# GLA mixer: the queries also in a PSUM bank, and the gates multiplied in ahead of the norm's root

## The chip, the cores and the metric

The kernel runs on one core of a Trainium2 chip. The metric is the device time of one launch in microseconds, the median of several. TensorE does the matrix products, VectorE, ScalarE and GpSimd the element-wise work, and SyncE issues the DMAs. SBUF is the working memory; PSUM has eight banks of 128 partitions x 512 floats, into which TensorE writes. GpSimd has no operand in PSUM anywhere in this kernel.

## The reference

Two layers over 1024 tokens of width 1024: layer 0 is gated linear attention (GLA), layer 1 a Mamba-2 mixer. Each is `x + mixer(rmsnorm(x))`, and one norm ends it. The change touches layer 0 alone. With four heads, key width 128 and value width 512 for each head:

```
q, k, v, g, gk_low = split(rmsnorm(x) @ w_in)
log_a = log_sigmoid(gk_low @ w_gate_up + b) / 16
per chunk:  b = cumsum(log_a)                       # decays, per key channel
  o = (q * exp(b)) @ S + (sum_d q_i k_j exp(b_i - b_j), j <= i) @ v
  S = exp(b_last) * S + (k * exp(b_last - b))^T @ v
o = rmsnorm(o, w_head_norm) * silu(g)               # per head, over 512
y = o @ w_out
```

The reference has chunks of 64; the kernel uses 128.

## The kernel before

Activations stand with features on partitions and 512 tokens on the free axis, so the work is done in four phases: `Gla(0)`, `Gla(1)`, `Ssd(0)`, `Ssd(1)`, each for one half of the tokens. The large products take every operand as a rounded part and a rest (`wh`/`wl` for weights, `hh`/`hl` for activations, `yh`/`yl` for a mixer's output) and three matmuls (`mm3`). They come in units of 12 matmuls with 512 columns, each with one 256 KB piece of weights. A piece is loaded, rounded by ScalarE (L171) and, on its first use, its rest is formed by GpSimd (`wl`, L176); that rest is stored, and in the second half of the tokens it is read back by a DMA (L174). Pieces are prepared four units ahead.

Beside the units run "sides", Python generators that are advanced by a rate per unit. `Gla.mixer(h)` is the side of head h: it runs beside the units of `gate(h)`, `outp(h-1)` and `qkv(h+1)`, some 28 of them, at 0.95 steps for each. Its stages are:

- the gate's projection into the bank `z` (L540), its log-sigmoid and scan into `b` (L551), and a copy of `b` into the bank (L553), read from there as `bz` and `zc`;
- the decay products: `kd`, `qd` (L567) and `d` (L572 to L576), and for three block sizes `keys(s)` (L582 to L584) and `queries(s)` (L600 to L607), where differences of `b` go through `Exp` and are multiplied by `k` or `q` (L584, L604). This stretch is called the decay stage below;
- the small products (L658) of keys and queries into four banks, placed into `at` under masks (L619, L623);
- the state updates and the outputs `o` (L699 to L723);
- the tail: squares of `o` (L729), the norm's root (`rstd_steps`, left in the bank `box[0]`), the gates' `Silu` (L736), the scaling by weight and root (L741), the product with the gate on GpSimd (L742), and the split into `yh` and `yl` (L746, L747), which `outp(h)` reads in the next head's units.

PSUM is two rings of four banks: `pp` for the units, `mb` for the mixers (`z`, the transposed keys `ptk`, the four product banks, states, outputs, the root). A unit's bank is emptied by `evac` functions behind the unit; that of `outp` adds it to `accs` on VectorE (L515). In `Gla(0)` the norm's root is applied as the banks are emptied, for the gates on VectorE too (L419).

The order of the instructions on each engine is not that of the Python program. It is fixed when the kernel is built: a planner walks through the instructions by priority (earlier in the program first) with its own estimates of times and of when buffers come free, and puts each on its engine's queue as its inputs are due. On the chip each queue then runs in that order, and an instruction that waits holds up all behind it.

Of the kernel before, what the change touches and what calls it, by code (L numbers as in the profile page):

```python
# [13 lines left out]
AF = mybir.ActivationFunctionType  # L14
ALU = mybir.AluOpType

P = 128
# [25 lines left out]
C_HN = C_GB + 4  # L43
# [10 lines left out]
def hybrid_kernel(ctx: ExitStack, tc: tile.TileContext, xT, w_in0, w_gk, w_up, w_out0,  # L54
                  w_in1, w_dt, w_out1, par, masks, tri, out):
    nc = tc.nc
    V, A, G, PE = nc.vector, nc.scalar, nc.gpsimd, nc.tensor
# [13 lines left out]
    def tl(tag, bufs, shape=(P, T), dt=F32):  # L71
        cnt[0] += 1
        return sb.tile(list(shape), dt, name=f"{tag}_{cnt[0]}", tag=tag, bufs=bufs)

    def ps(tag):
        cnt[0] += 1
        return (psp if tag == "pp" else psm).tile([P, T], F32, name=f"{tag}_{cnt[0]}", tag=tag)

    def tmp(n=P):
        t = tl("t", NTMP)  # L80
        return t[:] if n == P else t[0:n, :]

    def c3(ap, w=P):
        return ap.rearrange("p (n w) -> p n w", w=w)
# [5 lines left out]
    def act(out, in_, func, **k):  # L90
        name = SILU if func == AF.Silu else LN_EXP
        i = None
        if name != table[0]:
            i = A.preload_act_table_set(name)
            for m in table[2]:
                tc.add_manual_dep(i.ins, m.ins.name, ORDER, reason="table")
            table[:] = name, i, []
        o = A.activation(out, in_, func, **k)
        tc.add_manual_dep(o.ins, table[1].ins.name, ORDER, reason="table")
        table[2].append(o)  # L100
        return o
# [32 lines left out]
    def col(c, n=P):  # L134
        return pr[0:n, c:c + 1]
# [148 lines left out]
    def rstd_steps(ssum, n, box, var=None, stay=False):  # L284

        hi, lo = tl("t", NTMP, dt=F32R)[:], tl("t", NTMP, dt=F32R)[:]
        A.copy(hi, ssum)
        V.tensor_tensor(lo, ssum, hi.bitcast(F32), op=ALU.subtract)  # L290
        p = ps("mb")
        PE.matmul(p[:], onr[:], hi, start=True, stop=False)
        PE.matmul(p[:], onr[:], lo, start=False, stop=True)
        yield
        yield from rstd_of(p, n, box, var, stay)
# [19 lines left out]
    def square_into(ss, src, first, eng):  # L315
        if first:
            A.activation(ss, src, AF.Square)
        else:
            sq = tmp()
            A.activation(sq, src, AF.Square)  # L320
            eng.tensor_tensor(ss, ss, sq, op=ALU.add)  # L321
# [87 lines left out]
    class Gla:  # L409
# [115 lines left out]
        def mixer(self, h):  # L525
            t = self.t
            q, k = self.q[h], self.k[h]
# [20 lines left out]
            b = tl("m2", 1)[:]  # L548
            for c in range(NC):
                cs = slice(c * P, (c + 1) * P)  # L550
                V.tensor_tensor_scan(b[:, cs], m[:, cs], l[:, cs], 0.0, op0=ALU.add, op1=ALU.subtract)  # L551

            A.copy(z[:], b)  # L553
            bz, zc = z[:], c3(z[:])
            yield

            bc = c3(b)
# [6 lines left out]
            yield  # L564
            qd = tl("x", 4)[:]
            act(qd, bz, AF.Exp, scale=1.0 / 16)
            V.tensor_tensor(qd, q, qd, op=ALU.mult)  # L567


            d = tmp()  # L570
            dv = c3(d)
# [1 line left out]
            act(dv[:, :, 0:64], dv[:, :, 0:64], AF.Exp, scale=-1.0 / 16)  # L573
            act(dv[:, :, 64:P], dv[:, :, 64:P], AF.Exp, scale=1.0 / 16)
            V.tensor_tensor(dv[:, :, 0:64], c3(k)[:, :, 0:64], dv[:, :, 0:64], op=ALU.mult)
            V.tensor_tensor(dv[:, :, 64:P], c3(q)[:, :, 64:P], dv[:, :, 64:P], op=ALU.mult)  # L576

            def keys(s):

# [7 lines left out]
            def queries(s, e, c0=0, c1=NC):  # L587


                w, n = 4 * s, (c1 - c0) * P // (4 * s)  # L590
                own = 4 if s == 1 else 0
                e = e[:, 0:n * (6 * s + own)].rearrange("p (n w) -> p n w", n=n)
                cs = slice(c0 * P, c1 * P)
                bv, zv, qv = c3(b[:, cs], w), c3(bz[:, cs], w), c3(q[:, cs], w)
                after = []
                for i in range(3):
                    f, l = (i + 1) * s, 4 * s
                    o = sum(4 * s - (m + 1) * s for m in range(i))
                    after.append((e[:, :, o:o + l - f], f))
                    V.tensor_tensor(after[-1][0], zv[:, :, f:l], bv[:, :, f - 1:f].to_broadcast([P, n, l - f]),  # L600
                                    op=ALU.subtract)
                act(e[:, :, 0:6 * s], e[:, :, 0:6 * s], AF.Exp, scale=1.0 / 16)
                for o, f in after:
                    V.tensor_tensor(o, qv[:, :, f:4 * s], o, op=ALU.mult)  # L604
                if own:
                    G.tensor_copy(e[:, :, 6:10], qv)
                return e.rearrange("p n w -> p (n w)")  # L607

            def place(s, p, c0=0, c1=NC):
# [17 lines left out]
            for c in range(NC):  # L627
                cs = slice(c * P, (c + 1) * P)
                PE.transpose(ptk[:, cs], kd[:, cs], ident[:])

            o2 = [tl(tag, 1, (P, 2, T))[:] for tag in ("o0", "o1")]
            flat = [x.rearrange("p n w -> p (n w)") for x in o2]
            k16, q16 = keys(16), queries(16, flat[0])
            yield
            kh, kl = tl("ktok", 1, dt=F32R)[:], tl("t", NTMP, dt=F32R)[:]
            A.copy(kh, ptk[:])
            V.tensor_tensor(kl, ptk[:], kh.bitcast(F32), op=ALU.subtract)
            yield
            k4, q4 = keys(4), queries(4, flat[1])
            yield  # L640
            v = self.v[h]
            nst = NC - 1 if t == NT - 1 else NC

            def split(c):
                if c < nst:
                    vh, vl = tl("t", NTMP, dt=F32R)[:], tl("t", NTMP, dt=F32R)[:]
                    A.copy(vh, v[c])
                    G.tensor_tensor(vl, v[c], vh.bitcast(F32), op=ALU.subtract)  # L648
                    return vh, vl

            q1 = [queries(1, tl("raw", 2, (P, N_RAW))[:], 2 * i, 2 * i + 2) for i in range(2)]
            yield

# [37 lines left out]
            o = [o2[vb // 2][:, vb % 2, :] for vb in range(4)]  # L691
            def state(c, parts):
                if c < nst:
                    p = ps("mb")
                    cs = slice(c * P, (c + 1) * P)
                    mm3(p[:], kh[:, cs], kl[:, cs], *parts, True, True)
                    return p

            pst = state(0, vp)  # L699
            vp = split(1)  # L700
            yield
            for c in range(NC):
                cs = slice(c * P, (c + 1) * P)
# [24 lines left out]
            for vb in range(4):  # L728
                square_into(ss, o[vb], vb == 0, G)  # L729
                if vb % 2:  # L730
                    yield
            yield
            box = []
            yield from rstd_steps(ss, 512, box, stay=True)
            for g in self.g[h]:
                act(g, g, AF.Silu)  # L736
            yh, yl = [], []
            self.y[h] = yh, yl
            for vb in range(4):
                u = tmp()  # L740
                V.scalar_tensor_tensor(u, o[vb], col(C_HN + vb), box[0], op0=ALU.mult, op1=ALU.mult)  # L741
                G.tensor_tensor(u, u, self.g[h][vb], op=ALU.mult)  # L742
                yield
                a = tl("yh", 6, dt=F32R)[:]
                c = tl("yl", 6, dt=F32R)[:]
                A.copy(a, u)  # L746
                V.tensor_tensor(c, u, a.bitcast(F32), op=ALU.subtract)  # L747
                yh.append(a)
                yl.append(c)


    class Ssd:
# [456 lines left out]
    box = [[] for _ in ph]  # L1209
# [29 lines left out]
    for p in range(2):  # L1239
        g = ph[p]  # L1240
        for h in range(GH):
            o = [lambda: g.outp(h - 1)] if h else ([lambda: ph[0].outp(3)] if p else [])
# [162 lines left out]
```

## Time and profile before

| | |
|---|---|
| median of 3 runs | 1612.12 us (1608.9 to 1615.64) |
| the profiled execution | 1609.57 us, its span 1607.8 us |
| TensorE busy | 1570.2 us (98%) |
| VectorE, ScalarE, GpSimd busy | 951.4, 951.4, 655.3 us |
| DMA | 309 MB, 192 GB/s over the span |

The span is what the trace covers, and the profiled execution's own time is 1.8 us longer. `Gla(0)` takes the span up to some 400 us and `Gla(1)` up to some 750 us. In the rows, a letter and number such as L604 is the line of the kernel, names to the left of `<-` are written and those to the right read; `m` is the tag of `q`, `k` and `b`, `t` and `o` of scratch tiles, `mb` and `pp` of banks. A duration that is followed by xN in a timeline is that of N instructions merged.

### The profile page before, as it was taken

What the parts mean: (1) busy time and instruction counts of PE and PEld (TensorE: products, weight loads), DVE (VectorE), ACT (ScalarE), POOL (GpSimd) and SP (SyncE); (2) the same over time, 40 slices, a digit from 0 to 9 for tenths busy, and PEclk for the clock granted to TensorE, in tenths of its full rate; (3) what the DMA queues carried; (4) which work ended last, traced back from release to release, by engine and by line L of the source; (5) the groups of instructions that cost most, each with busy time, mean ns of one, the idle gap of its engine ahead of it and who ended that gap; (6) DMA issues with size and microseconds to landing.
All of it is one profiled execution on the core that took longest, in us unless ns stands there. A gap on an engine that the chain in (4) does not pass through costs nothing.

```text
span 1607.8 us, 24028 instructions
## 1 busy us (share of the span) xinstructions
PE 1570.2 (98%) x8272; PEld 1305.0 (81%) x8272; DVE 951.4 (59%) x1579; ACT 951.4 (59%) x1796; POOL 655.3 (41%) x542
## 2 busy tenths in 40 slices
PE   7999899999999999999999999999999999999996
PEld 5787787878888888888888888888778888888886
DVE  6357567495725446386735544457976963355657
ACT  4445363544636264564865767656657777667743
POOL 6456565643411021216536656565523222222322
PEclk9999999999999999999999999999999999999999
DMA  7545465464576456464586565566665766655752
GB/s 235 194 146 156 137 195 190 132 220 161 183 268 197 151 191 202 154 200 146 174 276 202 179 199 184 181 193 222 226 198 193 240 238 217 206 177 188 259 199 85
DMA packets 172747, 309.30 MB, mean 192 GB/s; under 512 B 19089, under 2 KB 25105, under 8 KB 172625
## 3 DMA queue, kind: packets, MB, share of 16 engines
q1 hardware_dynamic: 172624, 307.77, 58.6%
q8 instruction: 65, 1.06, 0.3%
q14 instruction: 58, 0.47, 0.1%
HBM read 232.06 MB, written 75.63 MB: 191 GB/s over the span
## 4 chain that ended last, share of the span: by engine, by line
PE 78%; DVE 11%; DMA 4%; ACT 4%; issue 1%; POOL 1%; SPq 0%; DVEq 0%; ACTq 0%; POOLq 0%
PE pp L223 18%; PE pp L224 18%; PE pp L225 18%; PE pp L469 3%; PE pp L470 3%; PE pp L471 3%; DMA wraw<-w_in 2%; PE mb L956 2%; PE mb L709 2%; PE mb L708 2%; PE mb L658 1%; PE mb L949 1%; DVE o L604 1%; PE mb L223 1%; PE mb L224 1%
## 5 line engine op out<-in xcount | busy, mean ns | idle before, releaser
L171 ACT CAST wh<-wraw 128x512 fp32r<-128x512 f32 x472 | 289.4, 618 | 343.1 <-PE pp L224 164.3
L223 PE MATMUL pp<-hh,wh 128*128 128x512 f32 x1184 | 468.5, 397 | 8.8 <-ACT wh L171 7.4
L224 PE MATMUL pp<-hl,wh 128*128 128x512 f32 x1184 | 464.0, 392 | 1.3 <-DVE hl L371 1.1
L225 PE MATMUL pp<-hh,wl 128*128 128x512 f32 x1184 | 463.0, 392 | 0.0
L176 POOL TENSOR_TENSOR wl<-wraw,wh 128x512 fp32r<-128x512 f32 x240 | 328.3, 1375 | 277.1 <-ACT wh L171 232.3
L223 PEld LDWEIGHTS pp<-hh,wh 128*128 128x128 f32 x1184 | 222.8, 188 | 60.3 <-ACT wh L171 9.0
L224 PEld LDWEIGHTS pp<-hl,wh 128*128 128x128 f32 x1184 | 223.0, 188 | 48.5 <-DVE hl L371 2.5
L225 PEld LDWEIGHTS pp<-hh,wl 128*128 128x128 f32 x1184 | 222.9, 188 | 46.2
L223 PE MATMUL pp<-yh,wh 128*128 128x512 f32 x448 | 177.9, 397 | 6.1 <-DVE acc L515 5.4
L225 PE MATMUL pp<-yh,wl 128*128 128x512 f32 x448 | 175.9, 393 | 0.0
L224 PE MATMUL pp<-yl,wh 128*128 128x512 f32 x448 | 175.4, 392 | 0.0
L321 POOL TENSOR_TENSOR ss<-ss,t 128x512 f32<-128x512 f32 x53 | 74.0, 1396 | 81.8 <-ACT t L320 70.4
L223 PEld LDWEIGHTS pp<-yh,wh 128*128 128x128 f32 x448 | 84.2, 188 | 26.1 <-issue 2.8
L469 PE MATMUL pp<-wh,hh 128*128 128x512 f32 x256 | 100.4, 394 | 2.7 <-DVE m L444 2.7
L470 PE MATMUL pp<-wl,hh 128*128 128x512 f32 x256 | 100.3, 392 | 0.0
L471 PE MATMUL pp<-wh,hl 128*128 128x512 f32 x256 | 99.7, 392 | 0.0
L225 PEld LDWEIGHTS pp<-yh,wl 128*128 128x128 f32 x448 | 84.3, 188 | 18.9 <-issue 0.2
L224 PEld LDWEIGHTS pp<-yl,wh 128*128 128x128 f32 x448 | 84.2, 188 | 17.8
L827 DVE SCALAR_TENSOR_TENSOR m<-pp,pr,m 128x509 f32<-128x509 f32 (+2 forms) x96 | 70.4, 743 | 42.8 <-ACT m L824 41.7
L827 DVE SCALAR_TENSOR_TENSOR x<-pp,pr,x 128x509 f32<-128x509 f32 (+2 forms) x96 | 71.2, 743 | 32.5 <-ACT x L824 31.4
L648 POOL TENSOR_TENSOR t<-v,t 128x512 fp32r<-128x512 f32 x28 | 38.1, 1371 | 112.6 <-DMA wraw<-w_in 28.9
L1038 POOL TENSOR_TENSOR t<-t,o 128x512 fp32r<-128x512 f32 x32 | 41.8, 1310 | 91.6 <-ACT o L1036 87.0
(286 smaller groups left out, 2623.7 us busy)
## 6 DMA issues: line engine op xcount, KB each, us to landing
wraw<-w_in SPq DMA_DIRECT2D x352, 256.0 KB, 3.5
low_in<-wl SPq DMA_DIRECT2D x176, 256.0 KB, 3.8
wl<-low_in SPq DMA_DIRECT2D x176, 256.0 KB, 3.2
wraw<-w_out SPq DMA_DIRECT2D x128, 256.0 KB, 3.5
low_out<-wl SPq DMA_DIRECT2D x64, 256.0 KB, 4.0
v<-a_cum SPq DMA_DIRECT2D x64, 256.0 KB, 3.8
wl<-low_out SPq DMA_DIRECT2D x56, 256.0 KB, 3.2
xn<-x SPq DMA_DIRECT2D x43, 256.0 KB, 3.8
```

The costliest lines, as they stand in the source:

```text
L171: A.copy(hi[:, 0:w], raws[n][:, 0:w])
L176: G.tensor_tensor(lo[:, 0:w], raws[n][:, 0:w], hi[:, 0:w].bitcast(F32), op=ALU.subtract)
L223: PE.matmul(o, lh, rh, start=first, stop=False)
L224: PE.matmul(o, lh, rl, start=False, stop=False)
L225: PE.matmul(o, ll, rh, start=False, stop=last)
L321: eng.tensor_tensor(ss, ss, sq, op=ALU.add)
L469: PE.matmul(o, rh[kb][:, cs], wh[:], start=(kb == 0), stop=False)
L470: PE.matmul(o, rh[kb][:, cs], wl[:], start=False, stop=False)
L471: PE.matmul(o, rl[kb][:, cs], wh[:], start=False, stop=(kb == KB - 1))
L648: G.tensor_tensor(vl, v[c], vh.bitcast(F32), op=ALU.subtract)
L827: V.scalar_tensor_tensor(dst[:, s:], o[:, 0:T - s], col(C_CW + j * 32 + si), dst[:, s:], op0=ALU.mult, op1=ALU.add)
L1038: G.tensor_tensor(xel[-1], xe, hi.bitcast(F32), op=ALU.subtract)
```

## The change

A second bank of the `mb` ring, `qz`, gets a copy of `q` from ScalarE just behind the copy of `b`. The products of `qd`, of the second half of `d` and of all `queries` read `qz` in place of `q`; GpSimd's copy of the queries' own columns (L606) still reads `q`. The `Silu` of the gates moves up, behind the first state product. The product with the gate moves ahead of the root's computation: GpSimd multiplies `o` into the gate's own tile. Behind the root, VectorE scales that tile by weight and root and writes the result `u` to a bank of the `mb` ring, from which ScalarE and VectorE make `yh` and `yl`.

```diff
             A.copy(z[:], b)
             bz, zc = z[:], c3(z[:])
+            qz = ps("mb")[:]
+            A.copy(qz, q)
             yield
...
             act(qd, bz, AF.Exp, scale=1.0 / 16)
-            V.tensor_tensor(qd, q, qd, op=ALU.mult)
+            V.tensor_tensor(qd, qz, qd, op=ALU.mult)
...
-            V.tensor_tensor(dv[:, :, 64:P], c3(q)[:, :, 64:P], dv[:, :, 64:P], op=ALU.mult)
+            V.tensor_tensor(dv[:, :, 64:P], c3(qz)[:, :, 64:P], dv[:, :, 64:P], op=ALU.mult)
...
-                bv, zv, qv = c3(b[:, cs], w), c3(bz[:, cs], w), c3(q[:, cs], w)
+                bv, zv, qv = c3(b[:, cs], w), c3(bz[:, cs], w), c3(qz[:, cs], w)
...
                 if own:
-                    G.tensor_copy(e[:, :, 6:10], qv)
+                    G.tensor_copy(e[:, :, 6:10], c3(q[:, cs], w))
...
             pst = state(0, vp)
             vp = split(1)
+            for g in self.g[h]:
+                act(g, g, AF.Silu)
             yield
...
+            for vb in range(4):
+                G.tensor_tensor(self.g[h][vb], o[vb], self.g[h][vb], op=ALU.mult)
             yield
             box = []
             yield from rstd_steps(ss, 512, box, stay=True)
-            for g in self.g[h]:
-                act(g, g, AF.Silu)
             yh, yl = [], []
             self.y[h] = yh, yl
             for vb in range(4):
-                u = tmp()
-                V.scalar_tensor_tensor(u, o[vb], col(C_HN + vb), box[0], op0=ALU.mult, op1=ALU.mult)
-                G.tensor_tensor(u, u, self.g[h][vb], op=ALU.mult)
-                yield
+                u = ps("mb")[:]
+                V.scalar_tensor_tensor(u, self.g[h][vb], col(C_HN + vb), box[0], op0=ALU.mult, op1=ALU.mult)
                 a = tl("yh", 6, dt=F32R)[:]
                 c = tl("yl", 6, dt=F32R)[:]
                 A.copy(a, u)
                 V.tensor_tensor(c, u, a.bitcast(F32), op=ALU.subtract)
                 yh.append(a)
                 yl.append(c)
+                yield
```

## Rows read from the trace of the kernel before

**Rows 1.** the page, part 1: busy us, share of the span, instructions

```profile
PE 1570.2 (98%) x8272; PEld 1305.0 (81%) x8272; DVE 951.4 (59%) x1579; ACT 951.4 (59%) x1796; POOL 655.3 (41%) x542
```

**Rows 2.** stretch, length, busy PE, PEld, DVE, ACT, POOL (x); PEclk, DMA share, GB/s

```profile
0.00:40.00 40.00, 28.30 (x103) 20.75 (x104) 28.01 (x37) 18.47 (x33) 25.54 (x27) 0.96 0.71 236
100.00:200.00 100.00, 93.92 (x512) 79.03 (x511) 58.09 (x100) 46.83 (x87) 56.21 (x44) 1.00 0.46 147
200.00:300.00 100.00, 97.46 (x492) 80.75 (x491) 62.70 (x104) 50.79 (x91) 56.40 (x44) 0.98 0.54 175
300.00:400.00 100.00, 97.98 (x507) 79.83 (x507) 70.80 (x116) 51.11 (x92) 46.44 (x35) 1.00 0.56 180
1570.00:1608.00 38.00, 25.57 (x205) 24.67 (x203) 25.78 (x51) 11.41 (x28) 9.24 (x11) 0.90 0.26 86
```

**Rows 3.** the same view, the second head's decay stage and the second half

```profile
130.00:172.00 42.00, 35.92 (x162) 28.68 (x162) 41.50 (x63) 24.42 (x43) 27.88 (x20) 1.00 0.54 163
500.00:700.00 200.00, 200.00 (x1033) 167.64 (x1032) 99.82 (x206) 107.98 (x199) 30.79 (x27) 1.00 0.56 182
```

**Rows 4.** what TensorE waited for, 40 to 480 us: total, times, longest

```profile
PE pp L223 <- DVE acc L515: 5.4, 3, 2.3
PE mb L658 <- DVE raw L604: 4.2, 2, 3.0
```

**Rows 5.** VectorE groups by shape, 40 to 480 us

```profile
L747 DVE TENSOR_TENSOR yl<-t,yh 128x512 fp32r<-128x512 f32 x16 | 19.4, 1249 | 1.6 <-ACT yh L746 1.6
L604 DVE TENSOR_TENSOR o<-m,o 128x384 f32<-128x384 f32 x10 | 12.6, 1257 | 0.0
L604 DVE TENSOR_TENSOR o<-m,o 128x256 f32<-128x256 f32 x10 | 12.0, 1205 | 0.0
L567 DVE TENSOR_TENSOR x<-m,x 128x512 f32<-128x512 f32 x5 | 6.5, 1297 | 0.0
L600 DVE TENSOR_TENSOR o<-mb,m 128x384 f32<-128x384 f32 x10 | 5.4, 544 | 0.0
L600 DVE TENSOR_TENSOR o<-mb,m 128x256 f32<-128x256 f32 x10 | 4.1, 407 | 0.0
L637 DVE TENSOR_TENSOR t<-mb,ktok 128x512 fp32r<-128x512 f32 x5 | 3.4, 677 | 6.0 <-ACT ktok L636 6.0
```

**Rows 6.** VectorE's timeline, second head: start, length, instruction

```profile
...
139.22 1.76 DVE L747 TENSOR_TENSOR yl<-t,yh 128x512 fp32r<-128x512 f32 x1
141.50 2.89 DVE L747 TENSOR_TENSOR yl<-t,yh 128x512 fp32r<-128x512 f32 x2
...
149.95 1.78 DVE L567 TENSOR_TENSOR x<-m,x 128x512 f32<-128x512 f32 x1
...
156.24 3.48 DVE L604 TENSOR_TENSOR o<-m,o 128x384 f32<-128x384 f32 x3
...
166.33 2.69 DVE L604 TENSOR_TENSOR o<-m,o 128x384 f32<-128x384 f32 x3
168.94 2.54 DVE L604 TENSOR_TENSOR raw<-m,raw 128x192 f32<-128x192 f32 x6
...
```

**Rows 7.** two lines, 480 to 720 us: ns min/median/max, starts, shapes

```profile
L604 DVE TENSOR_TENSOR o<-m,o x18: 273/412/549, 513.8 to 707.9; 128x384 f32<-128x384 f32 x6, 128x256 f32<-128x256 f32 x6, 128x128 f32<-128x128 f32 x6
L747 DVE TENSOR_TENSOR yl<-t,yh x12: 673/678/1749, 501.9 to 685.2; 128x512 fp32r<-128x512 f32 x12
```

**Rows 8.** third head: the busy view at 256, and the chain's product matmuls

```profile
256.00:257.00 1.00, 1.00 (x7) 0.59 (x8) 1.00 (x3) 0.51 (x1) 0.00 (x0) 0.50 1.07 375
...
171.63 3.06 PE mb L658 x56
...
256.42 4.17 PE mb L658 x56
```

**Rows 9.** groups by shape, whole span: writes to a bank

```profile
L313 DVE SCALAR_TENSOR_TENSOR mb<-t,t 128x512 f32<-128x512 f32 x8 | 5.6, 700 | 0.3
...
L553 ACT COPY mb<-m 128x512 f32<-128x512 f32 x8 | 4.7, 591 | 8.3 <-DVE m L551 8.3
```

## The prediction

> **What bounds the kernel now.** I first read the page's busy times: TensorE is busy 1570.2 us of a span of 1607.8, so 37.6 us of idle time are what a change of the other engines can win at most, beside what the clock gives [rows 1]. The view by stretches then says where they lie. The first 40 us hold 11.7 us of idle and the last 38 hold 12.4, and the change touches neither the start nor the end. From 100 to 400 us TensorE loses 6.1, 2.5 and 2.0 us, together 10.6, in the decay stages of the second, third and fourth head of the first token half [rows 2]. From 500 to 700 us, the same mixer code on the second half, it is busy for the whole 200 us [rows 3].
>
> The view of waits names what TensorE stood for: 5.4 us in three waits for the adds that empty the banks of `outp` (L515), and 4.2 us in two waits for the last products with the queries (L604) [rows 4]. Both are VectorE work, and VectorE was busy 41.5 of the 42 us of the second head's decay stage [rows 3]. So in these three stretches VectorE sets the pace, and TensorE stands because its queue holds an instruction that VectorE feeds too late.
>
> Why it is late is seen in the groups by shape. The products with `q` from SBUF (L604) take 1257 ns for 384 columns and 1205 for 256; the differences of the same shapes that read one input from a bank (L600) take 544 and 407 [rows 5]. The second half shows L604 itself at 412 median and at most 549 [rows 7]. What differs is GpSimd: busy 27.9 of 42 us in the slow stretch, 30.8 of 200 in the fast one [rows 3]. I read this as VectorE instructions with two SBUF inputs standing behind a GpSimd instruction, and those with one input in a bank not standing.
>
> **The change part by part.** *Reads of `q` from the bank.* Per head, two L604 of 384 columns go from 1257 to 544 ns, two of 256 from 1205 to 407, and L567 from 1297 to the 677 of L637, which has a bank input of that size [rows 5]: 1.43 + 1.60 + 0.62 = 3.6 us.
>
> *The split from the bank.* Four L747 per head go from 1249 to 677 [rows 5]: 2.3 us. Together a mean head saves 5.9 us of VectorE. For the second head the timeline gives more: three L747 took 1.76 + 2.89 against 3 x 0.68, L567 1.78 against 0.68, and the two triples of L604 3.48 + 2.69 against two times 0.544 + 0.407 + some 0.27 (the least of L604's own times, for the 128-column one) [rows 5 to 7]. That is 2.6 + 1.1 + 3.7 = 7.4 us, and I leave the 2.54 us of the six small ones as they are.
>
> A bound from below: GpSimd's work stays, so the collisions can land on the two-SBUF instructions that remain in the stage (L563, L575, two L584). Each could lose at most what L567 lost, 1.1 us, so 4.4 us come off: 3.0 us stay in the second head and 1.5 in a mean one. I take the upper value, because fewer such instructions meet fewer collisions.
>
> What may a bank cost by itself? L600 from a bank needs 544 ns for the shape that L604 does in at most 549 from SBUF when undisturbed [rows 5, 7], so I add nothing. The Trainium skill (Perfetto Trace Analysis, "Optimizing Scalar/DVE Operations") speaks against the change here: it gives VectorE about 60 ns of access overhead on SBUF and 125 on PSUM. By it, 22 operands a head moved to banks would cost an estimated 1.4 us, and the three heads' lower bound would fall from 6.0 us to 1.8; the trace doesn't agree, and the rest goes without it.
>
> *What TensorE gets back.* VectorE is the pace-setter only while it is late. The savings (7.4, and 5.9 in a mean head) exceed the standing time of each stretch (6.1, 2.5, 2.0) [rows 2], so the waits of 9.6 us [rows 4] should go; with the lower bounds 3.0 + 1.5 + 1.5 = 6.0 us go. What speaks most for the whole is the second half, where the planner made its order of the same code, GpSimd did little, and TensorE never stood [rows 3].
>
> *The clock.* After the third head's wait the granted clock was 0.50, the 1.2 GHz level, and the 56 product matmuls took 4.17 us against 3.06 in the second head [rows 8]. Without the standing, 1.1 us come back; nothing, if the wait stays.
>
> *The copy into `qz`.* One ScalarE copy of 0.59 us per head, as L553 [rows 9]. ScalarE is busy 24.4 of 42 us [rows 3], so its time is hidden; but the copy sits ahead of the `Exp` for `kd`, and I charge 0.6 us once, to the second head, where the saving is nearest to the need. With no cover it would be 0.6 in each of three heads, 1.8.
>
> *`Silu` and the gate's product.* Four `Silu` and four GpSimd products a head are moved, not added, and the activation table still changes twice a head: before, ahead of `Silu` and of the next head's `Exp`; now ahead of `Silu` and of the root's `Ln`. The tail loses the GpSimd product between L741 and L746, but `outp(h)` first reads `yh` behind the eight units of the next gate. At 1033 matmuls in 200 us [rows 3] its 96 matmuls last over 18 us, which hides the tail already: nothing won. The scaling into a bank stays at some 0.70 us, as L313 writes one [rows 9].
>
> *Waits that are added.* The `mb` ring has four banks. `qz` holds one from the copy to the last L604, for which the first products wait already, so the product banks come no later. But ScalarE's copy must wait for a free bank, and behind it on that queue stand the `Exp` for `kd` and the roundings of weights that TensorE needs; and each `u` needs a bank, behind which VectorE's next scan stands. No DMA is added or moved past a queue.
>
> The sum: 9.6 + 1.1 - 0.6 = 10.1 us off 1609.57 gives 1599.5. The profiled execution lies 2.55 us under the median of the runs, 1612.12; against that the forecast is 1602.
>
> **The rivals.** *The planner takes the saving.* It places the product matmuls by its own estimate of when they are due. If its estimate for VectorE shrinks as the chip's does, it moves them earlier and TensorE stands there again, for what its estimate lacks. For it: TensorE stood only 2.5 and 2.0 us in heads where VectorE lost some 5.9 [rows 2, 5], so much of the lateness already fell into slack of the order. Against it: the shapes stay the same, and collisions, which the order evidently missed, are what goes. It would win 3 to 7 us: 1605 to 1609, say 1607, which is also where the lower bounds (6.0 - 0.6) end.
>
> *Nothing is won.* The standing moves to the next late thing: with VectorE faster, the chain of `Exp` on ScalarE between L600 and L604 becomes the pace, or GpSimd's rests of weights. ScalarE was idle 17.6 of the 42 us [rows 3], which speaks against it. Time: 1610 to 1613, say 1612.
>
> *The banks run out (slower).* Place: the copy into `qz`, while the tail of the head before still holds the root's bank and the `u` banks. For it: a new holder for the whole decay stage in a ring of four, and two more kinds of writers that wait on it. Against it: the splits of the tail shown end at 144.4 us, and L567, which comes behind the copy, begins only at 149.95 [rows 6], so the banks should be free. Its price: the three L747 shown run from 139.2 to 144.4, 5.2 us. If `qz` stands for that long, the saving of 5.9 is just eaten and the time stays; that is the point from which it decides. At twice that, 10.4 us, the decay stage of three heads ends 4.5 us later than now, 13.5 us: 1626. The Trainium skill ("Identifying Performance Opportunities" of the same page) says that gaps that repeat on the engine that should be full can mean too little PSUM for the next tile; before, no such gap shows between 500 and 700 us.
>
> **How the numbers follow.** The forecast has 0.60, the planner 0.25, nothing won 0.09, banks 0.06. The forecast's own range is 1597 (all 10.6 us of idle time and 1.1 of clock off the lowest run, 1608.9) to 1605. The range for 8 in 10 is 1597 to 1610: it takes in the planner's case and half of nothing won, and leaves the banks out. A measurement of this kernel can tell about 0.5%, 8.1 us, from no change, so the bound is 1604.1. Of the forecast 0.54 lies under it; the rest, the planner's case and nothing won make 0.40; the banks 0.06.
>
> **What would show it.** Right: between 40 and 480 us TensorE no longer waits for L515 and L604; L604's 384-column mean falls from 1257 to about 545 and L747's to about 680; the stretches 100 to 400 us gain about 10 us of TensorE busy time; the clock stays at its upper level near 250 us. Wrong: the same waits with a shorter L604 (the planner); waits of the ScalarE copy or of the scaling for a bank, and of TensorE for the rounded weights (the banks); or L563, L575 and L584 longer by as much as L604 got shorter.

## The result and the profile after

The changed kernel takes 1596.51 us in the median of 6 runs (1595.66 to 1600.16), against 1611.46 (1608.9 to 1615.64) for the kernel before, also in 6 runs. The ratio is 0.9912, with a 95% interval of 0.99 to 0.9924: faster by 12 to 16 us. The forecast was 1602 with a range from 1597. The direction came as said (faster by over 0.5%), and the gain is larger than said: the median lies 0.5 us under the range's lower end, while the ratio, taken from the 1612.12 us that the forecast started from, gives 1597.9, just inside it. The profiled execution took 1597.23 us, 12.3 less than that of before. Executions at a lower granted clock are left out of all ratios here, and one kernel below (`after_no_rests`) has no profile but such a one, so it gets a time and no rows.

The page's busy times, to be read against [rows 1]: the span is 1595.5 us, so TensorE's idle time went from 37.6 to 29.0 us, and its busy time fell by 3.7.

```profile
PE 1566.5 (98%) x8272; PEld 1304.9 (82%) x8272; DVE 919.1 (58%) x1579; ACT 955.2 (60%) x1804; POOL 651.2 (41%) x542
```

Busy times by stretch, in the columns of [rows 2], for the three stretches where it stood:

```profile
100.00:200.00 100.00, 98.46 (x530) 82.75 (x530) 47.51 (x102) 49.05 (x90) 54.86 (x45) 1.00 0.50 156
200.00:300.00 100.00, 100.00 (x512) 83.69 (x512) 57.77 (x104) 51.69 (x93) 65.53 (x50) 1.00 0.59 182
300.00:400.00 100.00, 100.00 (x519) 82.17 (x519) 72.41 (x132) 59.09 (x105) 41.93 (x31) 1.00 0.62 193
```

TensorE's idle time there is 1.5 us in place of 10.6, and the granted clock is at its upper level in all three. What it still waited for between 40 and 480 us, against [rows 4]:

```profile
PE pp L223 <- DVE acc L515: 1.2, 1, 1.2
PE pp L223 <- ACT yh L748: 0.3, 1, 0.3
```

Nothing waits for the products with the queries any more, and the adds of L515 cost 1.2 us in place of 5.4. VectorE's groups by shape in the same stretch, against [rows 5]; L604 is L606 now, L567 is L569, L747 is L749, and L586 is the keys' product, which still has both inputs in SBUF:

```profile
L749 DVE TENSOR_TENSOR yl<-mb,yh 128x512 fp32r<-128x512 f32 x16 | 10.6, 684 | 0.8 <-ACT yh L748 0.7
...
L586 DVE TENSOR_TENSOR t<-m,t 128x512 f32<-128x512 f32 x10 | 8.7, 873 | 0.0
...
L606 DVE TENSOR_TENSOR o<-mb,o 128x384 f32<-128x384 f32 x10 | 5.5, 548 | 0.0
...
L606 DVE TENSOR_TENSOR o<-mb,o 128x256 f32<-128x256 f32 x10 | 4.1, 411 | 0.0
...
L569 DVE TENSOR_TENSOR x<-mb,x 128x512 f32<-128x512 f32 x5 | 3.4, 683 | 0.0
```

The products with the queries take 548 and 411 ns in place of 1257 and 1205, and the split 684 in place of 1249. The chain of work in the second and third head shows the 56 product matmuls at 3.02 us each; the third took 4.17 at the lower clock before [rows 8]:

```profile
175.19 3.02 PE mb L660 x56
...
255.99 3.02 PE mb L660 x56
```

One thing came differently. The second head's gate projection (L540) opens its mixer. It started at 130.15 us before and starts at 146.81 now, the first fence being TensorE's timeline of before and the second that of after:

```profile
130.15 0.39 PE L540 MATMUL mb<-stp,wup 128*128 128x512 f32 x1
```

```profile
146.81 0.39 PE L540 MATMUL mb<-stp,wup 128*128 128x512 f32 x1
```

Its products start at 175.19 us, against 171.63 before [rows 8]. So the time from the gate projection to the products shrank from 41 to 28 us in this head, and it starts 17 us later. The planner had made another order: the projection stands behind 104 matmuls of L223 on TensorE's queue, where it stood behind 80. The tail of the head before now overlaps little on VectorE with this stage: its last split starts at 149.82 us.

Landmarks in TensorE's timeline tell where the time came off. The products of the fifth head (the first of the second token half) started at 441.8 us before and at 429.7 after, 12.1 us earlier; the sixth to eighth lead by 12.1, 10.9 and 12.1, and the end by 12.3. All of it was won by the start of the fifth head's products.

### The profile page after: what moved, and what is told of

The parts are those of the page before. It is cut to its first block, busy times and chain, and to the rows that moved or that the text cites. A ratio compares the mean times of both kernels' runs of the same rounds, so it can differ in the third digit from the quotient of the medians.

```text
span 1595.5 us, 24009 instructions
## 1 busy us (share of the span) xinstructions
PE 1566.5 (98%) x8272; PEld 1304.9 (82%) x8272; DVE 919.1 (58%) x1579; ACT 955.2 (60%) x1804; POOL 651.2 (41%) x542
## 4 chain that ended last, share of the span: by engine, by line
PE 84%; DVE 5%; ACT 5%; DMA 4%; issue 1%; POOL 1%; SPq 0%; DVEq 0%; POOLq 0%; ACTq 0%
PE pp L223 20%; PE pp L224 20%; PE pp L225 20%; PE pp L469 4%; PE pp L471 4%; PE pp L470 4%; PE mb L713 2%; PE mb L712 2%; PE mb L959 2%; PE mb L660 2%; DMA wraw<-w_in 1%; PE mb L952 1%; DMA v<-a_cum 1%; PE mb L223 1%; PE mb L224 1%
## 5 line engine op out<-in xcount | busy, mean ns | idle before, releaser
L223 PE MATMUL pp<-hh,wh 128*128 128x512 f32 x1184 | 467.9, 396 | 8.7 <-ACT wh L171 7.6
L176 POOL TENSOR_TENSOR wl<-wraw,wh 128x512 fp32r<-128x512 f32 x240 | 322.5, 1352 | 313.2 <-ACT wh L171 245.0
L223 PEld LDWEIGHTS pp<-hh,wh 128*128 128x128 f32 x1184 | 222.7, 188 | 59.5 <-ACT wh L171 9.0
L223 PE MATMUL pp<-yh,wh 128*128 128x512 f32 x448 | 177.0, 397 | 2.6 <-DVE acc L515 1.2
L223 PEld LDWEIGHTS pp<-yh,wh 128*128 128x128 f32 x448 | 84.2, 188 | 22.3 <-ACT acc L889 2.4
```

The lines of the kernel that those rows point to most:

```text
L176: G.tensor_tensor(lo[:, 0:w], raws[n][:, 0:w], hi[:, 0:w].bitcast(F32), op=ALU.subtract)
L223: PE.matmul(o, lh, rh, start=first, stop=False)
```

## The experiments

Two theories stood at the start. *Theory 1*: VectorE's instructions with two SBUF inputs stand behind GpSimd, and the change takes the queries' products and the split out of that. *Theory 2*: the planner's new order did it. All ratios below are to the kernel before, each from four or more timed runs. Beside them stands where the products of the fifth head start in the profiled execution (441.8 us before, 429.7 after), since all of the gain is made by then.

**The parts alone.** The first run (`queries_only`) is the kernel before with the queries' part of the diff, its first five hunks:

```diff
+            qz = ps("mb")[:]
+            A.copy(qz, q)
...
-            V.tensor_tensor(qd, q, qd, op=ALU.mult)
+            V.tensor_tensor(qd, qz, qd, op=ALU.mult)
...
```

The second (`tail_only`) is the changed kernel without that part:

```diff
-            qz = ps("mb")[:]
-            A.copy(qz, q)
+            qz = q
```

> The first part alone: the copy into the bank and the reads of the queries from it; the tail as before. Theory 1 (VectorE's lateness comes from its two-SBUF instructions standing behind GpSimd, and the bank takes the queries' products out of that): L604 of 384 columns falls from 1257 to about 550 ns, some 3.6 us a head, TensorE's waits between 40 and 480 us fall from 9.6 to 2 to 4 us, and the time falls by 7 to 9 us, to about 1603. Theory 2 (the new order of the planner, not the reads, took the waits away): the waits can come out anywhere, with no tie to L604's duration.

> The second part alone: Silu and the gate's product ahead of the root, the scaled output in a bank; the queries read from SBUF. Theory 1: L604 stays near 1200 ns, the split of the output falls from 1249 to about 690 ns (2.3 us a head, ahead of the decay stage); waits of 5 to 7 us are left and the time falls by 3 to 5 us, to about 1607.5. Theory 2: the tail's new order brings most of the whole, 10 us or more.

The queries alone: 1598.5 us, ratio 0.9922 (0.9905 to 0.9939). VectorE's groups and TensorE's waits, 40 to 480 us:

```profile
L749 DVE TENSOR_TENSOR yl<-t,yh 128x512 fp32r<-128x512 f32 x16 | 19.5, 1240 | 1.7 <-ACT yh L748 1.6
...
L606 DVE TENSOR_TENSOR o<-mb,o 128x384 f32<-128x384 f32 x10 | 5.5, 547 | 0.4 <-ACT o L98 0.4
```

```profile
PE pp L223 <- ACT v L478: 1.5, 2, 0.8
PE pp L223 <- DVE v L480: 1.2, 1, 1.2
PE mb L660 <- DVE raw L606: 0.2, 1, 0.2
```

L606 is at 547 ns while the split stays at 1240, and none of the old waits is left but 0.2 us. That is more than theory 1 had priced (1603): the queries' reads alone are enough for nearly all. The fifth head's products start at 431.4 us, earlier by 10.4 of the 12.1 us. And theory 2 has no part in it: set side by side, the traces of the kernel before and of this run show the same order on TensorE and GpSimd from start to end, on VectorE but for six neighbouring instructions near 410 us, and on ScalarE, the added copy apart, up to 416 us.

The traces also show the collisions one by one, by what GpSimd was running when a product started. Of the ten L604 products of 384 columns before, seven started while GpSimd was in a subtraction (L176), and they took 1049 to 1654 ns; the other three took 544 to 548. In this run again seven of ten started so, and they took 542 to 558.

The tail alone: 1601.84 us, ratio 0.9941 (0.9925 to 0.9956), where theory 1 had 1607.5. The same two views:

```profile
L748 DVE TENSOR_TENSOR yl<-mb,yh 128x512 fp32r<-128x512 f32 x16 | 10.6, 685 | 0.8 <-ACT yh L747 0.7
...
L605 DVE TENSOR_TENSOR o<-m,o 128x384 f32<-128x384 f32 x10 | 7.9, 794 | 0.0
```

```profile
PE mb L223 <- DVE a L624: 2.4, 2, 1.8
PE pp L223 <- DVE acc L515: 1.1, 1, 1.1
PE pp L223 <- ACT yh L747: 0.4, 1, 0.4
```

The split fell to 685 ns as expected. But the queries' products, still from SBUF, fell to 794 ns too, and this nobody had expected. The trace says why: in this run's order only three of the ten started while GpSimd was in a product or subtraction, and those took 1051 to 1659 ns, the other seven 544 to 555. The parts don't add: 12.6 and 9.5 us by their ratios, and 14.2 together. Each shortens the same VectorE chain, and TensorE can't get back more than it had lost.

**Which half of the tail.** The `Silu` and the gate's product moved, the split not from a bank; `gate_early` is `tail_only` with:

```diff
-                u = ps("mb")[:]
+                u = tmp()
```

> The kernel before with Silu and the gate's product ahead of the root alone: the scaled output goes to an SBUF tile, the queries are read from SBUF. Of the 9.5 us that the whole second part brought: if the bank for the split is what counts, the split L747 stays near 1200 ns and the time falls by 2 to 4 us only, to about 1608; if moving GpSimd's four products out from between scaling and split is what counts, the split falls to 700 to 900 ns without the bank and the time is that of the second part, about 1601.

```profile
L748 DVE TENSOR_TENSOR yl<-t,yh 128x512 fp32r<-128x512 f32 x16 | 11.9, 766 | 0.0
...
L605 DVE TENSOR_TENSOR o<-m,o 128x384 f32<-128x384 f32 x10 | 9.0, 897 | 0.0
```

Measured: 1602.85 us, ratio 0.9942 (0.9927 to 0.9958), the same as with the bank. The rows (VectorE's groups) show the split at 766 ns without a bank. Before, the four GpSimd products ran between scaling and split, and 11 of the 16 splits started while GpSimd was running; here 3 of 16 do. So of the tail's edits the move of the `Silu` and of GpSimd's products counts (no run parts these two), and the bank for `u` has no effect that these runs can tell: the fifth head's products start at 434.5 us here and at 434.7 with the bank.

**Order or reads.** The bank is held as in the change and each engine's order of instructions is that of the changed kernel, but the reads for `qd`, `d` and the larger block sizes go to SBUF:

```diff
-            V.tensor_tensor(qd, qz, qd, op=ALU.mult)
+            V.tensor_tensor(qd, q, qd, op=ALU.mult)
...
-                bv, zv, qv = c3(b[:, cs], w), c3(bz[:, cs], w), c3(qz[:, cs], w)
+                bv, zv, qv = c3(b[:, cs], w), c3(bz[:, cs], w), c3((qz if s == 1 else q)[:, cs], w)
...
```

> The changed kernel with one thing taken back: the copy into the bank is made and the bank held as before, but qd, d and the queries of block sizes 16 and 4 read the SBUF tile; only those of size 1 read the bank. Each engine's order of instructions is that of the changed kernel. Theory 1: the L606 products of 384 and 256 columns go back to about 1.2 us, some 3.5 us a head, TensorE waits again for L515 or the products, 3 to 6 us in all, and the time lies 3 to 6 us above the changed kernel, at 1600 to 1603. Theory 2 (order alone): no difference to the changed kernel, 1596.5.

> The earlier kernel once more, for its profile. Theory 1: TensorE waits between 40 and 480 us for VectorE, 3 to 6 us, where the changed kernel, with the same order, waits 1.5; L606 of 384 columns near 800 ns (in the earlier profile 786).

Measured: 1601.36 us, ratio 0.9933 (0.9915 to 0.9951), and 1603.74 in one more, profiled execution (`bank_held_again`). Groups and waits of the latter:

```profile
L606 DVE TENSOR_TENSOR o<-m,o 128x384 f32<-128x384 f32 x10 | 7.9, 793 | 0.0
...
L569 DVE TENSOR_TENSOR x<-m,x 128x512 f32<-128x512 f32 x5 | 4.4, 880 | 0.0
```

```profile
PE pp L223 <- DVE acc L515: 2.4, 2, 1.2
PE mb L223 <- DVE a L625: 0.9, 1, 0.9
PE pp L223 <- ACT yh L748: 0.3, 1, 0.3
```

One place in the fifth head, the same three products (shown merged) behind the start of the same GpSimd subtraction, in the timelines of POOL and DVE, the first fence being after and the second this run:

```profile
421.36 1.76 POOL L176 TENSOR_TENSOR wl<-wraw,wh 128x512 fp32r<-128x512 f32 x1
421.87 1.08 DVE L606 TENSOR_TENSOR o<-mb,o 128x384 f32<-128x384 f32 x3
```

```profile
424.64 1.75 POOL L176 TENSOR_TENSOR wl<-wraw,wh 128x512 fp32r<-128x512 f32 x1
425.14 2.19 DVE L606 TENSOR_TENSOR o<-m,o 128x384 f32<-128x384 f32 x3
```

With the same order the products go from 548 to 793 ns, and TensorE waits 3.6 us in place of 1.5. Its timeline reaches the small products ahead of the second token half (L268) at 375.8 us, against 373.0 after, and the fifth head's products at 433.0 against 429.7: some 3 us for the reads alone. The timed intervals overlap, so the runs' times by themselves don't settle it. What the ratios say is that the rest of the change with its order keeps 0.0067 of 0.0088, and the trace that within this order the reads moved back cost some 3 us by the second token half. What this execution loses beyond that it loses behind 880 us, in `Ssd`, which the change doesn't touch. So the reads win in the old order (`queries_only`), and the new order wins without them, by letting fewer products start while GpSimd runs: 3 of 10 here too, in place of 7. Both ways take away the same collisions.

**GpSimd out of the way.** The rests of the weights are left out of both kernels, so the weights' low parts are zero; GpSimd fills zeros in place of a subtraction of two SBUF inputs:

```diff
-                G.tensor_tensor(lo[:, 0:w], raws[n][:, 0:w], hi[:, 0:w].bitcast(F32), op=ALU.subtract)
+                G.memset(lo[:, 0:w].bitcast(F32), 0.0)
```

> The kernel before, with GpSimd's subtraction for the weights' rests left out (a fill with zeros in its place, so the weights' low parts are zero). Theory 1: with GpSimd out of the way the same L604 from SBUF takes about 550 ns and L747 about 690, and the waits of 9.6 us between 40 and 480 us go, a gain of 9 to 12 us, about 1600. Rival (a bank is read faster than SBUF, GpSimd has no part): L604 stays near 1200 ns and the waits stay.

> The changed kernel with GpSimd's subtraction for the weights' rests left out (zeros in its place). Theory 1 (both the change and this take the same collisions away): the same time as the kernel before with the rests left out, 1590, within 2 us; the change has nothing left to win. Rival (the change wins through its order or through cheaper work, whatever GpSimd does): some 10 us below that, 1580.

The kernel before with this takes 1590.05 us, ratio 0.9875 (0.9854 to 0.9895), the fifth head's products at 424.4 us. Its groups and waits:

```profile
L604 DVE TENSOR_TENSOR o<-m,o 128x384 f32<-128x384 f32 x10 | 5.5, 551 | 0.1
...
L604 DVE TENSOR_TENSOR o<-m,o 128x256 f32<-128x256 f32 x10 | 4.2, 417 | 0.0
```

```profile
PE pp L268 <- ACT v L478: 2.0, 1, 2.0
PE pp L223 <- ACT v L478: 0.5, 2, 0.2
```

The very instructions that took 1257 and 1205 ns, with the same inputs in SBUF, now take 551 and 417, as from a bank. So a bank isn't faster; standing behind GpSimd was the slowness. The fills are shorter than the subtractions (527 ns in the mean against 1375), and only one of the ten products started during one (552 ns). But over the whole execution eleven VectorE products of 512 columns with two SBUF inputs started during a fill, and they took 670 to 745 ns: a fill holds up none. The waits for VectorE are gone without any of the change. (3.6 us of the gain were won ahead of the first head's L540, which starts at 65.6 us in place of 69.2.) The changed kernel with this takes 1588.09 us, ratio 0.9848 (0.9831 to 0.9864): its gain of 14.2 us shrinks to 2 by the medians and to 4 by the ratios, whose intervals overlap. The change wins what GpSimd's collisions had cost, by whichever of its parts, and what it wins beside that is at most these few us.

**A third bank.** The changed kernel with the keys in a bank too, read for `kd`, the first half of `d` and `keys`; also a test of the rival in which the banks run out:

```diff
+            kz = ps("mb")[:]
+            A.copy(kz, k)
...
-                V.tensor_tensor(e, k, e, op=ALU.mult)
+                V.tensor_tensor(e, kz, e, op=ALU.mult)
```

> The changed kernel with a third bank held through the decay stage: the keys are copied to a bank too and kd, d and keys read it. Banks theory (a full ring holds up ScalarE's copies and the weights behind them): with z, qz, kz and the transposed keys all four banks of the ring are taken, TensorE waits for rounded weights, several us slower than 1596.5. Theory 1: VectorE's last two-SBUF products (L586 at 873 ns) fall to about 680, but TensorE has only 1.5 us of waits left in this stretch, so 1595 to 1597, no difference.

```profile
L588 DVE TENSOR_TENSOR t<-mb,t 128x512 f32<-128x512 f32 x10 | 6.8, 679 | 0.0
```

```profile
PE pp L223 <- DVE acc L515: 1.4, 1, 1.4
PE pp L223 <- ACT yh L750: 0.3, 1, 0.3
```

1596.87 us, ratio 0.9908 (0.9892 to 0.9924), the fifth head's products at 429.8 us. The keys' products fall from 873 to 679 ns and the waits stay what they were. The copy into the third bank never stands. That into `qz` stands once, 1.3 us in the third head, for a split (L751) that empties a bank of the ring; after shows the same 1.3 us (for L749), and TensorE is busy throughout the stretch from 200 to 300 us in both. So even with all four banks taken a bank costs nothing that counts, and VectorE's further saving is worth nothing: TensorE has next to nothing left to wait for here.

**VectorE's work added back.** The changed kernel with two products of no use behind each `keys`, four in a decay stage, once with an input in the bank (`qz`, below) and once with both in SBUF (`q` in its place):

```diff
                 V.tensor_tensor(e, k, e, op=ALU.mult)
+                scr = tmp()
+                for _ in range(2):
+                    V.tensor_tensor(scr, qz, b, op=ALU.mult)
                 return e
```

> The changed kernel with four more VectorE products of 512 columns in each decay stage, into a scratch tile that nobody reads; one input is the bank qz. Theory 1, with the planner's order as its second half (work of VectorE that takes the time the planner counts on costs TensorE nothing, only lateness it doesn't count on does): the four take about 0.68 us each, 2.7 us a head, TensorE's waits between 40 and 480 us stay within 1 to 3 us, and the time stays at 1596 to 1599. Rival (VectorE's amount of work in the stage sets the pace): three heads lose 2.7 us each, 1604.

> The same four products in each decay stage, but with q in SBUF as the input, so both inputs lie in SBUF. Theory 1: they take 0.9 to 1.2 us each by collisions with GpSimd, 1 to 2 us a head beyond the one before, and since the order doesn't count on it TensorE waits for VectorE 3 to 6 us between 40 and 480 us: 1600 to 1603. Rival (amount of work): as the run with the bank, within 1 us.

With the bank: 1608.24 us, ratio 0.9986 (0.9975 to 0.9998). With SBUF: 1611.76 us, ratio 1.0009 (0.9995 to 1.0023); these intervals just overlap. Group and waits, the bank first:

```profile
L589 DVE TENSOR_TENSOR t<-mb,m 128x512 f32<-128x512 f32 x20 | 13.5, 675 | 0.0
```

```profile
PE pp L223 <- ACT yh L751: 3.1, 1, 3.1
PE pp L223 <- DVE acc L515: 1.3, 2, 1.0
```

```profile
L589 DVE TENSOR_TENSOR t<-m,m 128x512 f32<-128x512 f32 x20 | 20.8, 1038 | 0.0
```

```profile
PE pp L223 <- DVE acc L515: 4.6, 3, 2.2
PE pp L223 <- ACT yh L751: 3.1, 1, 3.1
```

The collisions cost what theory 1 says: the same instruction takes 1038 ns in place of 675, the wait for L515 grows from 1.3 to 4.6 us, and the fifth head's products start at 445.9 us in place of 442.3; the ratios lie 0.0023 apart. But the half of the theory that I had added, that work the planner counts on costs nothing, is refuted. Four products of 675 ns a head, 2.7 us, cost 11.7 us by the medians, nearly the whole gain. Part of it is waits of TensorE, 6.8 us between 40 and 480 us in place of 1.5, the longest that of 3.1 us for `yh`; part is a new order in which it spends longer on the small products of L268 (7.0 us busy against 3.8 after, 40 to 480 us). The remaining some 3 us are not accounted for. The rival (three heads at 2.7 us, 1604) was short of it as well.

## Why the prediction was right, and where its sizes were not

*What bounds.* Right: the standing time of 10.6 us from 100 to 400 us fell to 1.5, and by the view of waits it was VectorE's lateness that went.

*The reads from the bank and the split.* Right in price: 1257 to 548, 1205 to 411, 1297 to 683 and 1249 to 684 ns; forecast were 544, 407, 677 and 677. Right in cause for the queries, whose reads alone bring 547 in the old order. For the split the cause was mostly another: it fell to 766 ns without a bank, since GpSimd's products no longer run ahead of it. The lower bound, that collisions land on what remains, didn't come in the stage: the keys' product with two SBUF inputs fell from 1005 to 873 ns. Some landed elsewhere: of the eight scalings of the next norm (L350) five started beside a running GpSimd instruction in place of two, and their mean went from 812 to 1126 ns. The view of waits shows no stand of TensorE for them.

*No toll for a bank.* Right: 548 ns from the bank against 551 for the same product from SBUF with GpSimd's rests left out. The higher VectorE overhead on PSUM that the Trainium skill gives (Perfetto Trace Analysis, "Optimizing Scalar/DVE Operations") isn't seen in these products.

*What TensorE gets back.* The mechanism was right, and so was its largest term. The 401st matmul of L223 starts at 475.2 us before and at 463.2 after, 12.0 us earlier, and the span ends 12.3 earlier. Busy times up to there, before and after:

```profile
40.00:475.20 435.20, 424.07 (x2224) 350.66 (x2223) 264.85 (x471) 213.28 (x385) 210.25 (x162) 1.00 0.56 181
```

```profile
40.00:463.20 423.20, 421.66 (x2226) 350.42 (x2225) 234.13 (x471) 221.22 (x396) 207.37 (x163) 1.00 0.59 187
```

TensorE's idle time fell from 11.1 to 1.5 us, by the 9.6 of the forecast, and its busy time by 2.4, where the forecast had 1.1 for the clock and took 0.6 off. The clock's term was too small. Before, the granted clock was 0.50 not in the products alone, but over 3.4 us in which TensorE was busy all the while:

```profile
255.30:258.70 3.40, 3.40 (x22) 2.43 (x23) 3.40 (x9) 1.66 (x3) 0.99 (x1) 0.50 0.66 231
```

At half the clock these 3.4 us cost an estimated 1.7. The 0.6 for the copy was not spent. The rest may lie in how waits are recorded: matmuls of 512 columns start every 0.23 us (248.68, 248.91 and 249.13 us before) and are recorded as 0.39 long, so a stand of TensorE hides its first 0.16 us in the busy time of the matmul ahead, and the waits between 40 and 480 us went from nine to two. Over the whole span idle time fell by 8.6 and busy time by 3.7. The 14.2 us that the ratio gives agree with the traces' 12.3 within its interval (12 to 16).

*`Silu` and the gate's product: nothing won.* This step failed. I asked only whether `outp(h)` would wait for the tail. But the tail shares VectorE and GpSimd with the next head's decay stage, and moving the `Silu` and GpSimd's four products alone, with no bank, brought 1602.85 us. In the whole change this hides, since the queries' reads alone bring 1598.5.

*Waits that are added.* The wait of the copy for a bank came once, 1.3 us in the third head, and TensorE didn't stand for it; a third bank added none. The banks rival is out.

*The planner.* I feared that it would take part of the saving. With the queries' part alone it changed next to nothing. With the tail's part it did make a new order, and that order kept most of the gain even with the SBUF reads, because fewer of the queries' products start while GpSimd runs (3 of 10 in place of 7). That the tail of the head before is nearly done by then fits, but no run tests that by itself.

## What to carry to other kernels

When an elementwise instruction takes twice its least time in one half of a kernel and not in the other, look for what the neighbour engine does in the slow half before pricing the instruction itself: leaving that neighbour's work out for one run told the cause at once, and sorting the instruction's lengths by what the neighbour was running at its start tells it from a trace that is already there. Moving an operand to PSUM pays where it ends such a collision, and no more than the bounding engine really lost by it. Ask of a "hidden" tail not only who reads its result, but whose engines it occupies while the next stage runs.

## What the runs showed of the hardware that was not expected

A VectorE product of 512 columns with two SBUF inputs takes 1038 ns in the mean of 20 in `extra_sbuf`, and 675 with one input in a bank (`extra_bank`). The mean hides two kinds: the ten that started while GpSimd ran took 843 to 1782, the other ten 674 to 684. Such a product ends a fixed time behind GpSimd's instruction: in the kernel before the seven slow ones of 384 columns end 0.41 to 0.42 us behind it. GpSimd's fills with zeros, which have no SBUF input, hold up none of eleven (670 to 745 ns). This agrees with the Trainium skill (SBUF — State Buffer, "Who interferes with whom"), by which only a GpSimd instruction that reads SBUF holds up such a product. That so little as 2.7 us of VectorE work a head could cost 11.7 us, in a kernel where VectorE is busy 58% of the span, was not expected either.
